# Input projections of a convolution and retention block as Strassen block products over both sequence halves

## The chip, the cores and the metric

The kernel runs on one core of one Trainium2 chip. The metric is the device time of one launch in microseconds (us), the median of three runs. The engines are named as in the profile: PE (TensorE), DVE (VectorE), ACT (ScalarE), POOL (GpSimd) and SP (the engine that issues most of the transfers).

## What is computed

The input x has 1024 tokens of 1024 channels, all in float32.

```
h = rmsnorm(x) * norm_gain
a_val, a_glu, a_gate, q, k, v, r_gate, g_a, g_b = split(h @ w_in)      # 1024 x 11264
u = causal_conv31(a_val * sigmoid(a_glu)) + bias                       # per channel
y_a = (silu(layernorm(u)) * silu(a_gate)) @ w_conv_proj
o = retention(rotary(q), rotary(k) / 16, v)        # 4 heads, dk 256, dv 512, chunks of 128
y_b = (normalised per head(o) * gain * silu(r_gate)) @ w_ret_proj
out = rmsnorm(x + (sigmoid(g_a) * y_a + sigmoid(g_b) * y_b) @ w_out) * final_gain
```

Retention goes chunk by chunk: a chunk's output is its own masked scores times v, plus q times a state of 256 x 512, and the chunk's k and v then go into the state.

## The kernel before

Every float32 operand of a large product is split into two float32r parts, high and low: ACT copies the value to float32r (high), DVE or POOL subtracts that from the value (low). `mm3` (L107) makes one block product from three matmuls: high by high, high by low, low by high. A matmul has 128 rows, 128 columns of weights and 512 moving columns.

The sequence is worked in two halves of 512 tokens, one after the other (`Half`, L186). A half first holds h, transposed, as eight tiles of 128 channels in two parts. Then it goes through its four heads (`head`, L365): four groups of products for q and k (24 matmuls each, `proj_c`, L263), rotary on DVE (L296 to L299) and POOL (L300, L301), groups of the gated convolution input, the output projection of the head before (`ret_proj`, L553), v (`proj_t`, L273), and four chunks. Between two chunks stand the 24 matmuls of the gate r for the next one (`rg_part`, L532). After the heads come the gates, the layer norm, `conv_proj` and `out_proj`.

A weight tile is 128 x 1024 values, loaded by SP (L145) and split by ACT and DVE (L161, L162); each tile of w_in is loaded and split once per half. Products read h from SBUF and leave their results there: of the results only the state of each head goes to memory, between the halves.

The 31 taps of the convolution are DVE instructions on 512 columns (L347), queued in `taps` and let out a few at a time after each group of products (`flush`, L738 to L741). The groups are emitted in the order of the list `groups`; within that, a scheduler at build time fixes each engine's order by its own estimate of what is ready, so that neighbouring instructions of one engine can change places. At run time every engine and every queue goes through its instructions in that order, and waits at the first one whose inputs or buffers are not ready.

## Time and profile before

| | |
|---|---|
| time, median of 3 runs | 1478.68 us (1478.56 to 1479.04) |
| span of the profiled execution | 1477.6 us |
| PE busy | 1452.9 us, 98% |
| DVE busy | 1082.1 us, 73% |
| ACT busy | 519.3 us, 35% |
| POOL busy | 229.1 us, 16% |
| moved by DMA | 150.79 MB, 102 GB/s |
| granted PE clock | 0.999 of full speed |

Busy time is an average over the whole span. A busy PE can still be waiting inside: matmuls are pipelined and their ends are modelled, so the number of matmuls in a stretch says more than the busy time. In a row of merged instructions (x3, x24) the time runs from the start of the first to the end of the last; the distance from one start to the next is what an instruction costs its engine, and it is shorter than the duration shown.

### The profile page before, as it was taken

Reading aid. Unit: us, or ns where it says so; the run is one execution under the profiler, and the core shown is the slowest. Engines: PE = TensorE matmul, PEld = TensorE weight load, DVE = VectorE, ACT = ScalarE, POOL = GpSimd, SP = SyncE. Lnnn points to the kernel's source line nnn. Section 1 sums busy time; section 2 is a strip of 40 time slices with the busy share of each in tenths; the row PEclk is TensorE's granted clock in tenths of the full one; section 3 lists DMA queues with packets and bytes.
Section 4 is the critical chain, followed back from the end, with each engine's and each line's share of the span. In section 5 each row is a group of like instructions: output and inputs, shape, how many; then the busy total and the mean of one; then the engine's idle time right before and its main releaser. Section 6 shows DMA issues by size and latency. Waiting matters only on the chain.

```text
span 1477.6 us, 16740 instructions
## 1 busy us (share of the span) xinstructions
PE 1452.9 (98%) x6564; PEld 1203.5 (81%) x6564; DVE 1082.1 (73%) x1422; ACT 519.3 (35%) x696; POOL 229.1 (16%) x167
## 2 busy tenths in 40 slices
PE   7999999999999999999999999999999999999998
PEld 5788888888888888888888888878878888888886
DVE  4848986998898896436579969978677759944443
ACT  5333243234233243533332432342341441345321
POOL 0303102112100032120220030120020000311100
PEclk9999999999999999999999999999999999999999
DMA  8214332232231243333552132132331322432331
GB/s 292 81 62 136 107 114 86 72 114 67 91 114 58 71 140 104 99 99 101 213 181 76 55 103 91 52 108 67 97 94 64 114 72 72 131 110 95 93 126 57
DMA packets 43135, 150.79 MB, mean 102 GB/s; under 512 B 4784, under 2 KB 5424, under 8 KB 43056
## 3 DMA queue, kind: packets, MB, share of 16 engines
q1 hardware_dynamic: 40752, 143.43, 30.2%
q10 hardware_dynamic: 2304, 6.29, 1.1%
q8 instruction: 51, 0.84, 0.2%
q14 instruction: 28, 0.23, 0.1%
HBM read 143.41 MB, written 6.29 MB: 101 GB/s over the span
## 4 chain that ended last, share of the span: by engine, by line
PE 84%; DVE 10%; DMA 3%; issue 1%; ACT 1%; POOL 0%; SPq 0%; DVEq 0%; POOLq 0%; ACTq 0%
PE ps L105 83%; DVE cv L347 4%; DVE w L162 2%; PE ps L524 1%; DMA raw<-w_glu 1%; DMA xn<-x 1%; ACT w L161 1%; DMA x<-xT 0%; DVE phl L495 0%; DVE x L251 0%; DVE o L516 0%; PE ps L448 0%; DVE v L471 0%; DVE p L490 0%; DMA raw<-w_rg 0%
## 5 line engine op out<-in xcount | busy, mean ns | idle before, releaser
L105 PE MATMUL ps<-h,w 128*128 128x512 f32 x2688 | 620.4, 392 | 11.0 <-ACT h L229 11.0
L105 PEld LDWEIGHTS ps<-h,w 128*128 128x128 f32 x2688 | 504.8, 188 | 116.9 <-ACT h L229 11.0
L347 DVE SCALAR_TENSOR_TENSOR cv<-u,small,cv 128x512 f32<-128x512 f32 x480 | 365.0, 786 | 5.7
L105 PE MATMUL ps<-w,h 128*128 128x512 f32 x1536 | 357.4, 391 | 0.0
L161 ACT CAST w<-raw 128x1024 fp32r<-128x1024 f32 (+1 forms) x207 | 213.4, 1041 | 350.6 <-PE ps L105 226.6
L105 PEld LDWEIGHTS ps<-w,h 128*128 128x128 f32 x1536 | 286.6, 188 | 58.7
L162 DVE TENSOR_TENSOR w<-raw,w 128x1024 fp32r<-128x1024 f32 (+1 forms) x210 | 272.0, 1306 | 66.2 <-ACT w L161 65.5
L105 PE MATMUL ps<-oT,w 128*128 128x512 f32 x768 | 175.4, 389 | 0.0
L105 PEld LDWEIGHTS ps<-oT,w 128*128 128x128 f32 x768 | 144.2, 188 | 29.9
L105 PE MATMUL ps<-w,m 128*128 128x512 f32 x384 | 87.7, 390 | 0.0
L105 PE MATMUL ps<-u,w 128*128 128x512 f32 x384 | 87.4, 389 | 0.0
L105 PEld LDWEIGHTS ps<-u,w 128*128 128x128 f32 x384 | 72.1, 188 | 15.0
L105 PEld LDWEIGHTS ps<-w,m 128*128 128x128 f32 x384 | 71.9, 188 | 14.8
L511 DVE BATCH_NORM_STATS2 bs<-ps 128x6 f32<-128x512 f32 x32 | 22.3, 696 | 74.0 <-PE ps L105 73.8
L164 ACT ACTIVATE w<-raw,small 128x1024 fp32r<-128x1024 f32 x32 | 36.9, 1152 | 99.2 <-PE ps L105 63.9
L127 POOL TENSOR_TENSOR rr<-rs,neg_half 128x1 f32<-128x1 f32 (+1 forms) x34 | 19.7, 578 | 325.6 <-DVE rs L124 325.6
L165 DVE SCALAR_TENSOR_TENSOR w<-raw,small,w 128x1024 fp32r<-128x1024 f32 x32 | 47.7, 1492 | 17.9 <-ACT w L164 17.9
L494 ACT CAST phl<-p 128x512 fp32r<-128x512 f32 x48 | 29.8, 621 | 71.4 <-DVE p L490 45.2
L439 POOL TENSOR_TENSOR shl<-s,shl 128x512 fp32r<-128x512 f32 x8 | 12.1, 1517 | 263.4 <-ACT shl L438 175.5
L584 POOL TENSOR_TENSOR yb<-yb,g 128x512 f32<-128x512 f32 x16 | 30.4, 1914 | 120.7 <-ACT g L582 120.6
L624 DVE TENSOR_TENSOR cv<-cv,w_ag 128x512 f32<-128x512 f32 x16 | 11.1, 693 | 49.5 <-ACT w_ag L592 49.5
L627 POOL TENSOR_TENSOR u<-cv,u 128x512 fp32r<-128x512 f32 x16 | 29.0, 1816 | 98.2 <-ACT u L626 74.2
(109 smaller groups left out, 1118.3 us busy)
## 6 DMA issues: line engine op xcount, KB each, us to landing
raw<-w_v SPq DMA_DIRECT2D x32, 512.0 KB, 3.5
raw<-w_rg SPq DMA_DIRECT2D x32, 512.0 KB, 4.0
raw<-w_ret SPq DMA_DIRECT2D x32, 512.0 KB, 3.6
raw<-w_k SPq DMA_DIRECT2D x16, 512.0 KB, 3.6
raw<-w_glu SPq DMA_DIRECT2D x16, 512.0 KB, 3.7
raw<-w_val SPq DMA_DIRECT2D x16, 512.0 KB, 4.3
raw<-w_gb SPq DMA_DIRECT2D x16, 512.0 KB, 3.5
raw<-w_ga SPq DMA_DIRECT2D x16, 512.0 KB, 3.5
```

Source lines behind the costliest of these rows:

```text
L105: nc.tensor.matmul(ps, lhsT=l, rhs=r, start=start, stop=stop)
L127: nc.gpsimd.tensor_tensor(r[:, :n], s[:, :n], neg_half[:, :n], ALU.pow)
L161: nc.scalar.copy(w[:, 0, sl], t[:, sl])
L162: nc.vector.tensor_tensor(w[:, 1, sl], t[:, sl], w[:, 0, sl].bitcast(F32), ALU.subtract)
L164: nc.scalar.activation(w[:, 0, :], t, AF.Copy, scale=gain)
L165: nc.vector.scalar_tensor_tensor(w[:, 1, :], t, gain, w[:, 0, :].bitcast(F32), ALU.mult, ALU.subtract)
L347: nc.vector.scalar_tensor_tensor(o, u[:, k:k + T], cw[:, cb, k:k + 1], o, ALU.mult, ALU.add)
L494: nc.scalar.copy(hi[:, d, :], st["p"][:, d, :])
L511: nc.vector.bn_stats(stats, ps)
L524: nc.tensor.transpose(ps[:, e * P:(e + 1) * P], o[:, e * P:(e + 1) * P], ident)
L584: nc.gpsimd.tensor_tensor(y, y, g, ALU.mult)
L627: nc.gpsimd.tensor_tensor(u[:, 1, :], d, u[:, 0, :].bitcast(F32), ALU.subtract)
```

## The change

The product h @ w_in is done in a first phase for all 1024 tokens. A pair of weight tiles (256 output columns, or 128 of glu with 128 of val) with the two halves of the tokens and the two halves of the 1024 input channels makes a 2 x 2 block product. The Winograd form of Strassen's rule computes it in seven products of 12 matmuls instead of eight. Its sums of weight blocks are made per pair on DVE, those of h once at the start. Partial sums are seeded in PSUM: a product adds onto what ACT or DVE, or an earlier product, left in the bank.

There are 44 pairs. Their results (q and k after rotary, v, the gates after their activation, the convolution after its taps) are stored to memory. The taps now work on 1024 columns, 1.2 of them per product. In the second phase each half loads what it needs from there; v and the gate r come with channels in the partitions, so v is transposed on PE. The retention keeps its chunks, but the decay is applied to the scores' mask, to k and to q instead of in the rotary tables. `ret_proj` of the head before, and `out_proj` of the first half, are spread between the items of a head as fillers. The rms sums of h are taken from the transposed x with one-column matmuls.

```
+N_U = 32
+N_V = 8
+W_HEAD = 4
+W_CLOSE = 6
+SPLIT_AHEAD = 4
+TAPS_PER_SLOT = 1.2
...
+        def load(self):
+            self.N = U("N")
+            nc.sync.dma_start(self.N, a[self.n1[0]][self.n1[1]])
+            self.X, self.Y = U("X"), U("Y")
+            w = a[self.n2[0]][self.n2[1]]
+            nc.sync.dma_start(self.X[:, T:], w[:, :T])
+            nc.sync.dma_start(self.Y[:, :T], w[:, T:])
...
+            def split(x, names):
+                n = len(names)
+                hi, lo = U("wh", F32R, (P, n, T)), U("wl", F32R, (P, n, T))
+                x = x.rearrange("p (n t) -> p n t", t=T)
+                nc.scalar.copy(hi, x)
+                nc.vector.tensor_tensor(lo, x, hi.bitcast(F32), ALU.subtract)
...
+            def s1():
+                nc.vector.tensor_tensor(X[:, :T], X[:, T:], Y[:, :T], ALU.add)
+                split(N, ["A11", "A12"])
+            def s1_split():
+                w = U("ws", F32R, (P, 2, T))
+                nc.scalar.copy(w[:, 0, :], X[:, :T])
+                nc.vector.tensor_tensor(w[:, 1, :], X[:, :T], w[:, 0, :].bitcast(F32), ALU.subtract)
...
+            def g2():
+                self.G = U("G")
+                nc.vector.tensor_tensor(self.G.rearrange("p (n t) -> p n t", t=T), X.rearrange("p (n t) -> p n t", t=T),
+                                        N[:, :T].unsqueeze(1).broadcast_to([P, 2, T]), ALU.subtract)
+            def g2_split():
+                split(self.G, ["S2", "S3"])
+            def s4():
+                nc.vector.tensor_tensor(Y[:, T:], N[:, T:], self.G[:, :T], ALU.subtract)
+            def y_split():
+                split(Y, ["A22", "S4"])
...
+        def run(self, slot):
+            pa, px = psum(), psum()
+            def product(ps, w, h, seeded):
+                wh, wl = self.op[w]
+                for k in range(4):
+                    sl = slice(k * P, (k + 1) * P)
+                    hh, hl = hop[h][k]
+                    mm3(ps, wh[:, sl], wl[:, sl], hh, hl, k == 0 and not seeded, k == 3, seeded)
+            o1, o2 = U("o1", F32, (P, 2, T)), U("o2", F32, (P, 2, T))
+            s5 = o2[:, 1, :]
+            product(pa, "A11", "B11", False)
+            pb = psum()
+            nc.scalar.copy(pb, pa)
+            slot()
+            product(px, "S1", "T1", False)
+            nc.scalar.copy(s5, px)
+            slot()
+            product(pa, "S2", "T2", True)
+            pd = psum()
+            nc.vector.tensor_tensor(pd, pa, s5, ALU.add)
+            slot()
+            product(pb, "A12", "B21", True)
+            self.use.c11(pb, o1, o2)
+            slot()
+            product(pa, "S3", "T3", True)
+            nc.scalar.copy(px, pa)
+            nc.vector.tensor_tensor(s5, pa, s5, ALU.add)
+            slot()
+            product(pd, "S4", "B22", True)
+            self.use.c12(pd, o1, o2)
+            slot()
+            product(px, "A22", "T4", True)
+            self.use.c2(px, o1, o2)
+            slot()
...
+    class Rope:
+        def first(self, ps, o1, i):
+            cos, sin = cs[i][:, 0, :], cs[i][:, 1, :]
+            nc.vector.tensor_tensor(o1[:, i, :], ps, cos, ALU.mult)
+            nc.vector.tensor_tensor(self.m[i][:, 0, :], ps, sin, ALU.mult)
+        def second(self, x, o1, o2, i):
+            cos, sin = cs[i][:, 0, :], cs[i][:, 1, :]
+            nc.vector.tensor_tensor(self.m[i][:, 1, :], x, sin, ALU.mult)
+            nc.vector.tensor_tensor(o2[:, i, :], x, cos, ALU.mult)
+            nc.gpsimd.tensor_tensor(o1[:, i, :], o1[:, i, :], self.m[i][:, 1, :], ALU.subtract)
+            nc.gpsimd.tensor_tensor(o2[:, i, :], o2[:, i, :], self.m[i][:, 0, :], ALU.add)
...
+    for j in (0, 1):
+        normed(0, j)
+    h_split("B11", b11, nc.gpsimd)
+    for p in prep[:2]:
+        p()
+    for j in (0, 1):
+        normed(1, j)
+    sums(b11, b12, b11, ALU.subtract)
+    h_split("T1", b11, nc.vector)
...
+    for i, p in enumerate(pairs):
+        if i + 2 < len(pairs):
+            pairs[i + 2].load()
+        steps = deque(pairs[i + 1].prep() if i + 1 < len(pairs) else [])
+        def slot():
+            if steps:
+                steps.popleft()()
+            carry[0] += TAPS_PER_SLOT
+            flush(int(carry[0]))
+            carry[0] -= int(carry[0])
+        p.run(slot)
+    flush(len(taps))
...
+            def values(c0):
+                def go(w):
+                    for c in range(c0, c0 + 2):
+                        ps = psum()
+                        for e in range(4):
+                            nc.tensor.transpose(ps[:, e * P:(e + 1) * P],
+                                                st["vT"][e // 2][:, e % 2, c * P:(c + 1) * P], ident)
...
+            items = [(keys, 1.5), (values(0), 1), (values(2), 1)] + [(chunk(c), 3.4) for c in range(NC)]
+            fillers = list(fillers)
+            share = len(fillers) / len(items)
+            done = 0
+            for i, (f, cost) in enumerate(items):
+                add(f, cost=cost, limit=W_HEAD)
+                while done < len(fillers) and done < round((i + 1) * share):
+                    fillers[done]()
+                    done += 1
```

In the order of the pairs, a convolution pair stands ahead of every fourth other pair, eight times; per head come the pairs of k, q, v, v, and the two of the gate r. The layer norm's four steps stand among the fillers of the last head of a half, and its application between the eight parts of that head's `ret_proj`.

## Rows read from the trace of the kernel before

**Rows 1.** The page: span, and busy time of PE.
```profile
span 1477.6 us, 16740 instructions
PE 1452.9 (98%) x6564; PEld 1203.5 (81%) x6564; DVE 1082.1 (73%) x1422; ACT 519.3 (35%) x696; POOL 229.1 (16%) x167
```

**Rows 2.** Groups by line and shape: the products of w_in; count, busy, mean ns.
```profile
L105 PE MATMUL ps<-h,w 128*128 128x512 f32 x2688 | 620.4, 392 | 11.0 <-ACT h L229 11.0
L105 PE MATMUL ps<-w,h 128*128 128x512 f32 x1536 | 357.4, 391 | 0.0
```

**Rows 3.** ACT in time, gates of half 0: start us, duration us, instruction.
```profile
621.34 0.60 ACT L592 ACTIVATE w_ag<-ps 128x512 f32<-128x512 f32 x1 [2.39 <-PE ps L105]
...
643.10 0.60 ACT L592 ACTIVATE w_ag<-ps 128x512 f32<-128x512 f32 x1 [3.39 <-PE ps L105]
```

**Rows 4.** PE in time, from the start to its steady run.
```profile
10.97 21.21 PE L105 MATMUL ps<-h,w 128*128 128x512 f32 x78 [10.97 <-ACT h L229]
...
32.83 26.10 PE L105 MATMUL ps<-h,w 128*128 128x512 f32 x114
58.77 5.60 PE L105 MATMUL ps<-w,h 128*128 128x512 f32 x24
...
68.70 1.63 PE L105 MATMUL ps<-w,h 128*128 128x512 f32 x6
```

**Rows 5.** The chain that ended last: its first pieces with x and the row factors.
```profile
3.54 7.36 DMA x<-xT
...
22.41 1.03 POOL r L127
```

**Rows 6.** DVE in time: instructions back to back, of 512 columns and of 1024.
```profile
441.61 0.69 DVE L471 TENSOR_TENSOR v<-ps,v 128x512 fp32r<-128x512 f32 x1
442.21 0.74 DVE L347 SCALAR_TENSOR_TENSOR cv<-u,small,cv 128x512 f32<-128x512 f32 x1
442.87 0.69 DVE L471 TENSOR_TENSOR v<-ps,v 128x512 fp32r<-128x512 f32 x1
...
747.06 2.35 DVE L162 TENSOR_TENSOR w<-raw,w 128x1024 fp32r<-128x1024 f32 x2
...
753.27 1.22 DVE L162 TENSOR_TENSOR w<-raw,w 128x1024 fp32r<-128x1024 f32 x1
```

**Rows 7.** Groups by line and shape: taps, and a DVE instruction of their kind on 1024 columns.
```profile
L347 DVE SCALAR_TENSOR_TENSOR cv<-u,small,cv 128x512 f32<-128x512 f32 x480 | 365.0, 786 | 5.7
...
L165 DVE SCALAR_TENSOR_TENSOR w<-raw,small,w 128x1024 fp32r<-128x1024 f32 x32 | 47.7, 1492 | 17.9 <-ACT w L164 17.9
```

**Rows 8.** DVE and POOL in time where both read SBUF, and the same DVE instruction alone.
```profile
735.59 3.54 DVE L679 SCALAR_TENSOR_TENSOR res<-res,rv,fg 128x512 f32<-128x512 f32 x2
...
735.51 2.40 POOL L284 TENSOR_TENSOR csd<-cs,decay 128x1024 f32<-128x1024 f32 x1
...
745.72 1.42 DVE L679 SCALAR_TENSOR_TENSOR res<-res,rv,fg 128x512 f32<-128x512 f32 x2 [0.72 <-POOL rv L675]
```

**Rows 9.** Groups by line and shape: the first POOL subtraction of rotary.
```profile
L300 POOL TENSOR_TENSOR qk<-rp 128x512 f32<-128x512 f32 x16 | 20.7, 1293 | 113.8 <-DVE rp L298 106.4 <-issue 7.4
```

**Rows 10.** Busy time by stretch: PE, PEld, DVE, ACT, POOL, then clock, DMA share, GB/s.
```profile
360.00:460.00 100.00, 99.93 (x459) 82.85 (x458) 91.08 (x122) 28.88 (x35) 12.39 (x11) 1.00 0.32 100
```

**Rows 11.** All engines in time around the end of a chunk (state update, transposes, gate).
```profile
227.10 0.60 PE L524 MATMUL ps<-ident,o 128*128 128x128 f32 x4
227.32 0.68 DVE L490 SCALAR_TENSOR_TENSOR p<-p,ps 128x512 f32<-128x512 f32 x1
227.46 5.71 PE L105 MATMUL ps<-w,h 128*128 128x512 f32 x24
...
228.34 0.62 ACT L494 CAST phl<-p 128x512 fp32r<-128x512 f32 x1
228.63 1.29 DVE L495 TENSOR_TENSOR phl<-p,phl 128x512 fp32r<-128x512 f32 x2
```

**Rows 12.** PE in time at the end of the span.
```profile
1459.75 10.81 PE L105 MATMUL ps<-w,m 128*128 128x512 f32 x47
```

More of the change, by code (lines that the diff above doesn't have):

```diff
@@ L128, in rsqrt, with flush @@
         return r
+    taps = deque()
+    def flush(n):
+        while taps and n > 0:
+            taps.popleft()()
+            n -= 1
+    nc.gpsimd.memset(ones, 1.0)
+    nc.gpsimd.memset(invd, 1.0 / D)
+    nc.gpsimd.memset(neg_half, -0.5)
+    zero = const("zero", [P, P], F32R)
+    nc.gpsimd.memset(zero.bitcast(F32), 0.0)
+    zrow = sb.tile([P, T], F32R, tag="t", bufs=N_T, name="zrow")
+    nc.gpsimd.memset(zrow.bitcast(F32), 0.0)
+    for _ in range(8):
+        mm(psum(), zero, zrow, True, True)
@@ new lines, in hybrid_block_kernel, with h_split @@
+    pairs = []
+    for i, p in enumerate(rest):
+        if i % 4 == 0 and i // 4 < NK:
+            cb = i // 4
+            pairs.append(Pair(("w_glu", cb), ("w_val", cb), Conv(cb)))
+        pairs.append(p)
+    hop = {}
+    v_left = [N_V]
+    def h_split(name, xs, eng):
+        ks = []
+        for x in xs:
+            if v_left[0] > 0:
+                v_left[0] -= 1
+                t = V("h", (P, 2, 2, T))
+                hi, lo = t[:, 0], t[:, 1]
+            else:
+                hi, lo = U("h", F32R, (P, 2, T)), U("h", F32R, (P, 2, T))
+            nc.scalar.copy(hi, x)
+            eng.tensor_tensor(lo, x, hi.bitcast(F32), ALU.subtract)
+            ks += [(hi[:, k, :], lo[:, k, :]) for k in range(2)]
+        hop[name] = ks
@@ new lines, in hybrid_block_kernel @@
+    for j in range(4):
+        load_x(0, j)
+    nc.sync.dma_start(small, a["small"])
+    nc.sync.dma_start(ident, a["ident"])
+    for j in range(4):
+        load_x(1, j)
+        if j == 1:
+            pairs[0].load()
+    cs = []
+    r_rows = []
+    for hf in range(2):
+        ps = psum()
+        for j in range(4):
+            q = U("sq", F32, (P, 2, T))
+            nc.scalar.activation(q, xt[hf][j], AF.Square, scale=D ** -0.5)
+            for k in range(2):
+                for c in range(NC):
+                    mm(ps[:, c:c + 1], q[:, k, c * P:(c + 1) * P], ones[:, 0:1],
+                       j == 0 and k == 0 and c == 0, j == 3 and k == 1, True)
+        r4 = rsqrt(ps[:, :NC], NORM_EPS, NC)
+        mm(ps, zero, zrow, True, True)
+        r_rows.append(bcast_rows(r4))
@@ new lines, in hybrid_block_kernel @@
+    sums(b21, b21, b11, ALU.subtract)
+    h_split("T4", b21, nc.vector)
+    for i in range(2):
+        t = U("cs", F32, (P, 2, T))
+        nc.sync.dma_start(t, a["cs"][i])
+        cs.append(t)
+    nc.sync.dma_start(dmask, a["dmask"])
+    nc.sync.dma_start(xi, a["xi"])
+    pairs[1].load()
+    carry = [0.0]
+    for i, p in enumerate(pairs):
[9 more added lines that the diff above has]
+        p.run(slot)
@@ L703, in finish @@
[L703 to L706 removed]
+            return lambda: add(go, [("w_out", 4 * eh + kp, None) for kp in range(4)] if c == 0 else [],
+                               4 if c == NC - 1 else 0)
     halves = [Half(0), Half(1)]
[L709 to L710 removed]
+    late = []
     for hv in halves:
+        hv.m, hv.res, hv.u2, hv.ss = [], [], [], []
@@ L719, in hybrid_block_kernel @@
+            hv.head(h, fill)
+        todo = list(range(NK))
+        for g in hv.ret_proj(H - 1):
+            if todo:
+                add(lambda w, hv=hv, cb=todo.pop(0): hv.ln_apply(cb), cost=0)
+            g()
+        for j in range(4):
+            hv.gate_b(j)
+        for db in range(NK):
+            hv.conv_proj(db)
+        late = [hv.out_proj(eh, c) for eh in range(2) for c in range(NC)]
+    for g in late:
+        g()
     for g in groups:
         ws.seq += g.weights
-    carry = 0.0
```

649 lines of the change are left out of this document (267 added, 382 removed).

## The prediction, made before the changed kernel was built or run

> **What bounds the kernel now.** I read the page first: PE is busy for 1452.9 of 1477.6 us [rows 1]. Busy time alone doesn't say that PE works at its pace, so the second view is the groups by line and shape, for the number of matmuls: the products of w_in are 2688 + 1536 = 4224 of 512 columns [rows 2], and the code makes 1968 others of that shape (768 in `ret_proj`, 384 each in `conv_proj` and `out_proj`, 432 in the chunks). The third is ACT in time where it does nothing but take results of `proj_c`: five gates start over 21.76 us, so 24 matmuls take 5.44 us and one takes 0.2267 us [rows 3]. Then 6192 matmuls are 1403.7 us of the 1477.6. PE's matmul count is the bound. The remaining 73.9 us hold the start, the small products and transposes, the waits between and the tail. At the start the 216 matmuls issued before 68.70 us would take 49.0; with some 4 us of small products PE has lost about 16 us by then [rows 4]. After its last matmul at 1470.56 the span lasts 7 us more [rows 12]. The rest of the span has little idle time; even in a stretch of 100 us in which DVE is busy for 91.1, PE goes on at its pace, with 459 records in 99.9 us [rows 10].
>
> So a cut in matmuls comes off the end, as long as nothing else takes its place. The change cuts matmuls and gives DVE, the next engine, a larger and a tighter part.
>
> **Products removed.** 44 pairs by 7 by 12 are 3696 matmuls in place of 4224: 528 fewer, 528 x 0.2267 = -119.7 us. A product of 12 takes 2.72 us, a pair 19.04, the phase 838.
>
> **Transposes of v.** 32 chunks each gain four of 128 columns. Four of the same kind delay the next product from 227.10 to 227.46, 0.36 us [rows 11]: 32 x 0.36 = +11.5 us.
>
> **Start.** Before, PE begins at 10.97 with h not yet normed [rows 4]. Now the seven sums of h must be made first, and pair 0 can't end before the last of them (T4). x is there from 10.9 us, and the row factors were known at 23.4 before [rows 5]; with sums of squares by one-column matmuls I take 20 for the first half. From there DVE has 16 normings of 512 columns at 0.66, 8 sums and 8 low parts of 1024 at 1.13, and the seven preparations of pair 0, 6.3 us (below): 35 us. The prices are the distances between starts: 0.60 for 512 columns, 0.66 with a scalar from a tile, 2.35 - 1.22 = 1.13 for 1024 [rows 6]. Three of the seven operands have their low parts on POOL, six of 2.40 us [rows 8]. While POOL reads SBUF, DVE's instructions with two SBUF inputs stretch: a couple takes 3.54 us instead of 1.42 beside a POOL instruction of 2.40 [rows 8]. I put 10 of these 14.4 us on DVE's path, since the normings take one input from PSUM. T4 is then ready at about 65 and pair 0 ends at 66, where 19 were its due: 47 lost instead of 16, +31 us. The ends: without collisions and with a first product overlapping, 37 lost (+21); with factors at 23.4 and every collision paid, 56 (+40).
>
> **DVE in the first phase.** A pair costs DVE four instructions of 1024 (low part of N, the sum G, its low part, low part of Y) and three of 512 (two sums, low part of S1), 4 x 1.13 + 3 x 0.60 = 6.32, plus two additions on partial sums, 1.20: 7.52 us. Taps come at 1.2 x 7 = 8.4 a pair while there are any, 31 last 3.7 pairs out of five. A tap of 1024 columns isn't in the trace. From below it is 0.66 + 0.53 = 1.19; 0.76 busy per tap now (365.0/480) gives 1.29; the like instruction on 1024 has a mean of 1.49 [rows 7]. I take 1.25: 10.5 us a pair. A plain pair with taps is 18.0 us of DVE against 19.04 of PE. It fits, and what hides it is that six of the seven products leave time between the sums that PE waits for. PE's tight point is `pd`: product five may not write the bank until DVE has added `s5`, so a DVE behind by more than 2.72 - 0.60 = 2.1 us stops PE.
>
> The eight rotary pairs don't fit: 8 x 0.60 = 4.8 more on DVE, and four POOL instructions of 1.29 [rows 9], 5.2 us in which DVE's two-input work may stand. k and q come one after the other and meet taps in all four heads. At the full price a pair is 7.52 + 10.5 + 4.8 + 5.2 = 28.0, 9 too many; two in a row less the slack of 2.1 are 15.9, and 12.6 for the two heads where the taps run out in q: 57 us in all. With half of POOL's time it is 36; the other end is 0, if the order of the queues lets PE take products of the next pair. I take +23: the stretch of rows 10, where a DVE at 91% held nothing up, is nearer than the full price, though its load is an average and this comes in lumps.
>
> The Trainium skill (SBUF — State Buffer, "SBUF: two separate sides") says that the port pair DVE and GpSimd share is an exclusive lock for a whole instruction, so that the loser blocks. Rows 8 bear that out: 2.12 of 2.40 us came on DVE. By that rule alone the rotary pairs would cost 57 us instead of 23; it is the sharper part of the second rival.
>
> **Transfers.** Each pair loads 1 MB and stores 1 MB (convolution pairs half), 88 MB or so in 850 us, no more per us than now (102 GB/s). Loads are issued two pairs ahead, some 19 us, so I cost them at nothing. On SP's queue they stand behind stores that wait for a pair's last results, at most one pair; the cover goes if buffers run short. By my count the 32 U buffers are just full at a pair's start (h 12, cos and sin 2, two pairs of loads 6, operands 7, results 4, convolution 1), so the next operands wait for the stores before, some 6 us, and still have 10 to spare.
>
> **Second phase.** PE has about 505 us of work. Four things take the place of the products that hid the rest. (a) Between kv and the next chunk's product with the state PE had 24 matmuls. The state takes from the kv's end to 228.63 + 1.29 = 229.92, 2.8 us after PE went on at 227.10 [rows 11], 3.2 with the two halves in one instruction. Fillers are 2.72 each, but none stands between chunks 0 and 1: 2.5 us x 6 heads, and 3 gaps in the first head of all, which has no fillers: 22. (b) That head also waits for its first loads, 5. (c) At six head changes four w_ret tiles are split at once, when the last filler has let go of them; 2 each, 12. (d) The layer norm stands beside a head's full DVE load: its 15 subtractions and sums are 9 us of DVE, seven sums on POOL another 9, chained; 8 a half, 16. Together 55; the build-time order can move ready products forward, as it does now, which I credit with 10, and the waits that were in the middle before go, about 10. Net +35, with ends of +5 (all gaps filled) and +70 (nothing filled, the layer norm at twice that).
>
> **Sum**, on the profiled execution: 1477.6 - 119.7 + 11.5 + 31 + 23 + 35 = 1458.4. The median of the runs is 1.1 us above the span: 1459.5, so 1460 us. With every term at its better end it is 1396, at its worse end 1537.
>
> **Rivals.**
> (1) The gaps close: the build-time order pulls ready products into every wait. For it: the 99.9 us in rows 10. Against: the start can't be filled. Start +25, rotary 0, second phase +12: 1407 us. Chance 0.22.
> (2) DVE becomes the bound of the first phase, and the change is slower. Place: the pairs with taps. It decides from a tap of (19.04 - 7.52)/8.4 = 1.37 us on. At 1.49 [rows 7] a plain pair is 20.0, 1 us over for some 26 pairs, 26; with rotary at its full 57 the phase loses 83 instead of 23: 1520 us, or 1500 with a tap at the edge. For it: rows 8, and DVE's largest share yet. Against: taps are cheaper than 1.37 wherever they are alone. Chance 0.20.
> (3) The second phase opens up: the state's chain, the weights and the layer norm at +75 instead of +35: 1500 us. For it: no long run of independent products is left in a head. Against: fillers, and a whole `out_proj` in the second half's first head. Chance 0.13.
> That the products aren't saved is no rival: the count is in the code.
>
> **Chances.** My forecast's case, 1435 to 1485, has 0.45. A difference of 0.2% (3 us) is about what can be told from none. Of the forecast's case 0.39 is faster by more than that, 0.05 the same, the rest slower; with rival 1, faster 0.61, with a little of 2 and 3 the same 0.06, slower 0.33. The range is 1405 to 1515: it leaves out the better end of rival 1 and the worse of 2.
>
> **What would show it.** Right: 3696 matmuls of the pairs at 0.227 us between results; pair 0 ending near 66 us; PE idle mostly in the first 66 us, in the eight rotary pairs, and at heads' chunk 0 and layer norm. DVE near 95% in pairs with taps, behind 80% after the last tap. Wrong: PE below 90% across plain pairs (rival 2); results of a pair more than 19.1 us apart without DVE busy, which would mean buffers or loads; idle PE above 70 us in the second phase (rival 3), or below 20 (rival 1).

## The result, and the profile after

The changed kernel takes 1574.52 us (median of four runs, 1573.98 to 1577.29) where the kernel before takes 1478.62: 1.0653 times as long, 95% interval 1.0638 to 1.0668. It is slower by 96 us; 1460 with a range of 1405 to 1515 was forecast. The profiled execution, the slowest of the four, has a span of 1575.5 us, 117 more than the 1458.4 of the sum.

The page of the changed kernel: span, busy time by engine, and three of its groups (busy us, mean ns, idle time before and its releaser).

```profile
span 1575.5 us, 16585 instructions
PE 1451.7 (92%) x6278; PEld 1168.9 (74%) x6278; DVE 1184.5 (75%) x1378; ACT 545.8 (35%) x761; POOL 215.6 (14%) x153
...
L108 PE MATMUL ps<-h,wh 128*128 128x512 f32 x2112 | 669.2, 398 | 31.1 <-DVE ps L234 13.4
...
L108 PE MATMUL ps<-h,wl 128*128 128x512 f32 x1056 | 418.7, 396 | 2.6 <-DVE wl L183 2.6
L333 DVE SCALAR_TENSOR_TENSOR cv<-u,small,cv 128x1024 f32<-128x1024 f32 x240 | 313.0, 1304 | 3.3
```

Against [rows 1], PE's busy time is the same with fewer matmuls, and its share fell from 98% to 92%. The products are there as counted: 2112 + 1056, and 528 more with S1, are the 3696 of the sum [rows 2]. A tap lasts 1.304 us in the mean, below the 1.37 from which rival 2 decides; DVE's share is 75% over the span and 89% in the stretch with the first taps and rotary pairs (100 to 200 below), so no long stretch has it as its bound. So the time went to three other places, which the stretches show (columns as in [rows 10]):

```profile
0.00:100.00 100.00, 70.02 (x233) 56.10 (x234) 58.23 (x62) 34.92 (x37) 25.52 (x19) 0.81 0.29 102
100.00:200.00 100.00, 92.73 (x391) 74.06 (x390) 89.08 (x90) 29.56 (x41) 16.33 (x9) 0.97 0.26 90
...
700.00:900.00 200.00, 200.00 (x869) 162.81 (x868) 158.27 (x159) 75.96 (x111) 0.00 (x0) 1.00 0.30 106
...
953.00:1576.00 623.00, 544.17 (x2444) 435.06 (x2442) 438.44 (x612) 213.20 (x301) 128.00 (x96) 0.94 0.42 142
```

**The start.** PE in time (start, duration, instruction, idle time before):

```profile
5.58 13.81 PE L108 MATMUL ps<-ones,sq 128*128 128x1 f32 x64
...
23.66 13.65 PE L108 MATMUL ps<-ones,sq 128*128 128x1 f32 x64
...
43.83 2.04 PE L108 MATMUL ps<-dg,ones 128*128 128x512 f32 x2 [5.48 <-DVE dg L119]
...
73.79 0.79 PE L108 MATMUL ps<-h,wh 128*128 128x512 f32 x1 [6.84 <-POOL h L374]
...
82.58 0.79 PE L108 MATMUL ps<-h,wh 128*128 128x512 f32 x1 [3.73 <-ACT wh L182]
87.88 1.22 PE L108 MATMUL ps<-h,wh 128*128 128x512 f32 x2 [4.50 <-DVE ps L234]
```

The one-column matmuls (the first two rows) of the two halves run one after the other, so the second half's row factors reach PE at 43.83; after that PE stands for the low parts on POOL (6.84), for a weight tile's high part on ACT (3.73) and for the first partial sum (L234, 4.50). The first product of pair 1 ends at 101.46, so pair 0 ends at about 98.7 and not at 66: some 80 us are lost where 47 were forecast. About 3 of them belong to this execution: in five of the variants below whose start is the same (x_align, x_fill, x_rope, x_noln, x_notap) that product ends at 98.6 to 99.0. What DVE and POOL do at that time, one fence for each engine:

```profile
57.99 2.36 DVE L408 TENSOR_TENSOR x<-x,x 128x1024 f32<-128x1024 f32 x2
...
65.77 2.36 DVE L408 TENSOR_TENSOR x<-x,x 128x1024 f32<-128x1024 f32 x2
...
73.77 6.68 DVE L408 TENSOR_TENSOR x<-x,x 128x1024 f32<-128x1024 f32 x2 [2.23 <-POOL h L374]
80.37 4.50 DVE L374 TENSOR_TENSOR h<-x,h 128x1024 fp32r<-128x1024 f32 x2
...
87.14 0.69 DVE L234 TENSOR_TENSOR ps<-ps,o 128x512 f32<-128x512 f32 x1
```

```profile
65.10 17.56 POOL L374 TENSOR_TENSOR h<-x,h 128x1024 fp32r<-128x1024 f32 x4 [21.89 <-ACT h L373]
```

The first and the last of these four on POOL by themselves:

```profile
65.10 8.63 POOL L374 TENSOR_TENSOR h<-x,h 128x1024 fp32r<-128x1024 f32 x1 [21.89 <-ACT h L373]
...
79.33 3.33 POOL L374 TENSOR_TENSOR h<-x,h 128x1024 fp32r<-128x1024 f32 x1
```

Two sums of 1024 columns on DVE take 2.36 us with POOL idle (57.99). The four low parts on POOL take 17.56 us together, 4.39 each in the mean and not the 2.40 of [rows 8], and it isn't always DVE that pays. POOL's first one lasts 8.63 us: while it is open, DVE goes through sums and low parts at their usual price (65.77) and pauses at 71.5, and PE waits for what POOL makes there. From 73.77 on DVE pays: its next two sums, for which PE is waiting too, take 6.68.

**The pace.** ACT in time, the copies that follow product one of three plain pairs:

```profile
782.29 0.57 ACT L227 COPY ps<-ps 128x512 f32<-128x512 f32 x1 [2.19 <-PE ps L108]
785.15 0.59 ACT L230 COPY o<-ps 128x512 f32<-128x512 f32 x1 [2.29 <-PE ps L108]
...
801.66 0.57 ACT L227 COPY ps<-ps 128x512 f32<-128x512 f32 x1 [4.91 <-PE ps L108]
...
821.03 0.57 ACT L227 COPY ps<-ps 128x512 f32<-128x512 f32 x1 [2.19 <-PE ps L108]
```

A pair takes 19.37 us, with PE busy all the time at full clock (the stretch from 700 to 900), and not 19.04. Products one to four take about 2.80 us each, five to seven 2.72.

**The second phase.** It begins at 953.60 and lasts 621.9 us. What PE waited for in it (us in total, times, longest us):

```profile
PE ps L640 <- DVE o L633: 17.1, 12, 4.3
PE ps L108 <- POOL acc L709: 15.6, 2, 9.1
PE ps L108 <- DVE oT L648: 9.9, 5, 3.6
PE ps L108 <- ACT v L584: 9.5, 1, 9.5
PE ps L108 <- DVE dg L119: 8.5, 2, 4.2
```

None of these waits is longer than 9.5 us, and no engine is full: DVE is busy for 438 of 623 us, PE for 544. The waits name short chains (a chunk's normed output o, the layer norm's sum and row factors, the values of v in the first head) and each stands where PE has nothing else next in its queue.

### The profile page after: what moved, and what is told of

Its sections match the earlier page's. It is cut to its first block, busy times and chain, and to the rows that moved or that the text cites. A ratio compares the mean times of both kernels' runs of the same rounds, so it can differ in the third digit from the quotient of the medians.

```text
span 1575.5 us, 16585 instructions
## 1 busy us (share of the span) xinstructions
PE 1451.7 (92%) x6278; PEld 1168.9 (74%) x6278; DVE 1184.5 (75%) x1378; ACT 545.8 (35%) x761; POOL 215.6 (14%) x153
## 4 chain that ended last, share of the span: by engine, by line
PE 48%; DVE 7%; issue 3%; POOL 3%; DMA 1%; ACT 1%; SPq 0%; POOLq 0%; DVEq 0%; ACTq 0%
PE ps L108 47%; DVE w L485 1%; POOL acc L709 1%; DVE o L633 1%; POOL rr L129 1%; PE ps L640 1%; DVE p L603 1%; DVE bs L628 1%; DVE acc L723 1%; DVE phl L612 1%; PE ps L581 0%; DMA raw<-w_ret 0%; POOL q L566 0%; DVE oT L648 0%; DMA gb<-gb_d 0%
## 5 line engine op out<-in xcount | busy, mean ns | idle before, releaser
L108 PE MATMUL ps<-h,wh 128*128 128x512 f32 x2112 | 669.2, 398 | 31.1 <-DVE ps L234 13.4
L108 PEld LDWEIGHTS ps<-h,wh 128*128 128x128 f32 x2112 | 401.4, 191 | 130.2 <-DVE ps L234 16.8
L108 PE MATMUL ps<-h,wl 128*128 128x512 f32 x1056 | 418.7, 396 | 2.6 <-DVE wl L183 2.6
L333 DVE SCALAR_TENSOR_TENSOR cv<-u,small,cv 128x1024 f32<-128x1024 f32 x240 | 313.0, 1304 | 3.3
L108 PEld LDWEIGHTS ps<-h,wl 128*128 128x128 f32 x1056 | 200.9, 190 | 48.5 <-DVE wl L183 3.1
L108 PEld LDWEIGHTS ps<-oT,w 128*128 128x128 f32 x768 | 148.0, 196 | 53.6 <-DVE oT L648 11.3
L108 PE MATMUL ps<-h,ws 128*128 128x512 f32 x528 | 133.0, 400 | 2.6 <-ACT h L373 1.6
L108 PEld LDWEIGHTS ps<-h,ws 128*128 128x128 f32 x528 | 100.5, 191 | 27.8 <-ACT h L373 2.1
L183 DVE TENSOR_TENSOR wl<-G,wh 128x1024 fp32r<-128x1024 f32 x44 | 53.8, 1223 | 48.1 <-ACT wh L182 48.1
L183 DVE TENSOR_TENSOR wl<-N,wh 128x1024 fp32r<-128x1024 f32 x44 | 55.9, 1270 | 30.6 <-ACT wh L182 19.2
L182 ACT CAST wh<-N 128x1024 fp32r<-128x1024 f32 x44 | 46.2, 1049 | 55.6 <-POOL o L291 48.7
```

Source lines behind the costliest of these rows:

```text
L108: nc.tensor.matmul(ps, lhsT=l, rhs=r, start=start, stop=stop, skip_group_check=onto)
L182: nc.scalar.copy(hi, x)
L183: nc.vector.tensor_tensor(lo, x, hi.bitcast(F32), ALU.subtract)
L333: nc.vector.scalar_tensor_tensor(o, u[:, k:k + S], cw[:, cb, k:k + 1], o, ALU.mult, ALU.add)
```

## The experiments

The times are medians; ratios are to the kernel before, which ran beside them (1477.7 to 1478.8 us). Edits are to the changed kernel unless it is said otherwise.

**x_eight: the products alone.** A pair by the eight plain products, in the same two phases.
```diff
-            product(pa, "A11", "B11", False)   # seven products, sums between
+            product(px, "A21", "B12", True)    # eight products, no sums
+            product(px, "A22", "B22", False)
...
```


> The changed kernel with the pairs' seven products replaced by the plain eight (no sums of blocks of h or of the weights, everything else as in the changed kernel, taps at 1.05 a product so that a pair gets as many). Theory 'the products are saved, the phases cost': each pair is one product longer, 44 x 2.77 = 122 us, less some 20 us of the start without sums and some 20 of the rotary pairs, which DVE then has time for: 1640 to 1665 us. Rival 'the sums eat the saving': the seven-product form with its sums takes about as long as eight plain products; then 1560 to 1600 us.

1656.02 us, 1.1195 [1.1174, 1.1215]: 81.5 us more than with seven. Its plain pairs take 22.40 us, eight times 2.80, against 19.37. 44 times 3.03 is 133 us of products saved; some 50 of them go back where the eight products lose less: 28 in the start (pair 0 ends at 73.7 with one product more) and 22 in the rotary pairs, which all take 22.40. With as many products as the kernel before it is 178 us slower than that: this is what the two phases cost with nothing saved.

**x_align and x_phase: the pace.** x_align makes the tiles behind the small parameters begin at multiples of 128 bytes; x_phase places two small groups of tiles ahead of U.
```diff
-    small = const("small", [P, N_SMALL])
+    small = const("small", [P, N_SMALL + 8])       # x_align
+    for tag in ("rs", "rr"):                       # x_phase, ahead of U's first tile
+        pre = sb.tile([P, NC], F32, tag=tag, bufs=6, name=f"{tag}_pre")
```


> The changed kernel with 32 more bytes per partition in the table of small parameters, so that the tiles behind it start at multiples of 128 bytes, as they did before the change. In the changed kernel the four products of a pair that take h from the V tiles last 2.80 us and the three that take it from U tiles 2.73. Theory 'address': these tiles' start address slows the matmuls; then all seven take 2.72, which is 44 x 4 x 0.07 = 12 us, and some 6 more in conv_proj and out_proj: 1555 to 1560 us. Rival 'place or traffic': what slows them is where V lies or what goes on beside it; then nothing moves, 1573 to 1577 us.

1575.82 us, 1.0656 [1.064, 1.0672], pairs still 19.37 us: alignment was not it.

> Two small groups of tiles (384 bytes in all) are placed ahead of the U tiles instead of between the U and the V tiles, so that the distance from U to V in SBUF becomes 131,072 bytes, a multiple of 4096, as it was in the kernel before (126,976). Nothing else changes. Theory A (products are slower, 2.80 us per 12, because the low bits of the addresses of the two operands differ): products one to four of a pair fall from 2.80 to 2.72 us, conv_proj and out_proj from 44.95 to 43.6 us per 192; a plain pair 19.37 to 19.1; 12 us less in the first phase, 5 in the second: 1555 to 1560 us. Rival (the pace has another cause, such as the number of stores and loads beside it): 1573 to 1577 us, 2.80 as before.

1562.96 us, 1.0566 [1.0541, 1.0591]. ACT in time in x_phase, at the copies after product one (L230 here):

```profile
775.15 0.57 ACT L230 COPY ps<-ps 128x512 f32<-128x512 f32 x1 [2.12 <-PE ps L108]
...
794.19 0.57 ACT L230 COPY ps<-ps 128x512 f32<-128x512 f32 x1 [4.84 <-PE ps L108]
...
813.23 0.57 ACT L230 COPY ps<-ps 128x512 f32<-128x512 f32 x1 [2.12 <-PE ps L108]
```

19.04 us to the hundredth, in the plain pairs away from rotary. The last pair's first product ends 9.8 us earlier (927.47 for 937.23), the span is 12.8 shorter: the distance of the two groups of tiles sets the pace, as theory A has it, and the median came 3 us above its range. Which low bits of the addresses count isn't shown.

**x_start and x_start2: the start.**
```diff
-                    mm(ps[:, c:c + 1], q[:, k, c * P:(c + 1) * P], ones[:, 0:1], ...)  # 64 a half
+                nc.vector.tensor_tensor(qs, qs, q, ALU.add)                           # then 4 a half
-    h_split("B11", b11, nc.gpsimd)        # B21 and B22 too
+    h_split("B11", b11, nc.vector)
+            if i == 0 and first_steps:    # x_start2: one sum of h after each product
+                first_steps.popleft()()
```


> The changed kernel with the squares of a half summed on DVE before the one-column matmuls (4 products of them in place of 32 a half), and with the low parts of B11, B21 and B22 on DVE instead of POOL. Theory 'late row factors': the start is long because PE takes 14 us for the squares of each half one after the other, so that the second half's factors come at 44 us, and because POOL and DVE then block each other; pair 1's first product would end near 72 us in place of 101.5, and the kernel takes 1543 to 1550 us. Rival 'DVE's own chain of sums': DVE's work for the seven operands binds, and taking POOL's 14 us on adds what the factors save; then 1565 to 1575 us.

1563.24 us, 1.0573 [1.0556, 1.0591]. Pair 1's first product ends at 87.78. DVE in time in x_start, its last pieces before product five may go on:

```profile
68.03 1.21 DVE L411 TENSOR_TENSOR x<-x,x 128x1024 f32<-128x1024 f32 x1
69.16 2.47 DVE L374 TENSOR_TENSOR h<-x,h 128x1024 fp32r<-128x1024 f32 x2
71.55 0.68 DVE L188 TENSOR_TENSOR X<-X,Y 128x512 f32<-128x512 f32 x1
72.15 1.22 DVE L183 TENSOR_TENSOR wl<-N,wh 128x1024 fp32r<-128x1024 f32 x1
73.28 0.68 DVE L194 TENSOR_TENSOR ws<-X,ws 128x512 fp32r<-128x512 f32 x1
73.89 0.69 DVE L234 TENSOR_TENSOR ps<-ps,o 128x512 f32<-128x512 f32 x1
```

Without POOL a low part takes 1.2 us, but DVE is one solid chain, and the partial sum (L234) stands behind all of it: products five to seven come after the whole preparation.

> x_start (squares summed on DVE ahead of one matmul per column block, low parts of B11, B21 and B22 on DVE) with one more edit: the sums of h and their low parts are issued one after each product of pair 0, and pair 1's preparation after pair 0's last product, so that the addition on the first partial sum (pd), for which product five waits, stands in DVE's queue in its turn and not behind the whole chain. Theory: in x_start PE stood idle from 54 to 74 us for that order alone; pair 1's first product ends 8 to 12 us earlier than in x_start (87.78), at 76 to 80, and the time is 1551 to 1556 us. Rival: DVE's work of the start is one solid chain whatever its order, pair 1's first product ends at 86 to 89 and the time is 1562 to 1565.

1561.6 us, 1.0564 [1.0549, 1.058]. Pair 1's first product ended at 79.85, as the theory had it, and pair 43's at 922.11 against 923.31 in x_start. 7.9 us were gained and 6.5 of them had gone back by pair 4, most likely because the work put off was still DVE's.

**x_rope, x_notap and x_slack: taps and rotary.**
```diff
-            carry[0] += TAPS_PER_SLOT
+            carry[0] += 0.3 if isinstance(p.use, Rope) else 1.15                  # x_rope
-            taps.extend(tap(k) for k in range(1, TAPS))                           # x_notap
-            pd = psum()
+            pe, pd = psum(), psum()                                               # x_slack
+            nc.scalar.copy(pe, pa)
             nc.vector.tensor_tensor(pd, pa, s5, ALU.add)
-            product(pa, "S3", "T3", True)
+            product(pe, "S3", "T3", True)
```


> First phase only: 0.3 taps per product in the eight rotary pairs and 1.15 in the others, instead of 1.2 in all until they run out; the number of taps is the same. Theory (22 us of the first phase are lost where rotary and taps come together on DVE): the first phase ends 12 to 20 us earlier than 953.6 and the time is 1555 to 1563 us. Rival (the eight rotary pairs lose time to their own chain, POOL and partial sums, and not to taps): the first phase ends within 4 us of 953.6, 1571 to 1577 us.

1578.32 us, 1.0684 [1.0666, 1.0702]: no gain. The build-time order put more of the taps in threes on DVE (3.9 us in a piece, 29 such groups for 21); the losses moved to other pairs and kept their sum, 836.3 us from pair 1 to pair 43 for 835.8. So this run doesn't settle the theory.

> 30 of the 31 taps of the convolution are left out (its first multiplication and the stores stay), so DVE has 240 instructions of 1.30 us less in the first phase. In the changed kernel the 42 pairs after the second lose 22 us, all within three pairs of a rotary one. x_rope spread the taps otherwise, but at build time they were grouped in threes, so it settled nothing. Theory (the 22 us come where taps and rotary meet on DVE): 5 us or less are left of the 22, and the time is 1552 to 1560 us. Rival (the rotary pairs' own chain, with POOL and the partial sums, costs them with no taps at all): 15 us or more are left, 1567 to 1576 us.

1551.64 us, 1.0503 [1.0485, 1.052]. From pair 1 to pair 43 every pair takes 19.36 to 19.38 us, the rotary ones too; the stretch from 100 to 200 us, which had 391 matmuls, in x_notap:

```profile
100.00:200.00 100.00, 100.00 (x435) 81.35 (x435) 55.28 (x66) 32.93 (x47) 14.33 (x9) 1.00 0.31 105
```

With POOL's rotary work still there and no taps, nothing is lost: all of the 22 us came from rotary and taps together.

> One edit to the changed kernel: ACT copies the bank of product three to another bank, product five goes on there, and DVE's addition of the first partial sum (pd) reads the old bank. Product five then waits for ACT and no longer for DVE; pd is first needed by product six, one product (2.7 us) later. Theory (the 22 us of the rotary pairs are lost at pd, for which product five waits): 10 to 18 us less, 1557 to 1565 us. Rival (DVE has more work than fits beside the rotary pairs, and PE waits for it at the next place): under 5 us less, 1570 to 1577 us.

1560.52 us, 1.0559 [1.0543, 1.0575]: 14 us less, inside the theory's range, but the trace gives the theory less than half of the 22. What PE waited for from pair 1 to pair 43, first the changed kernel, then x_slack:

```profile
PE ps L108 <- DVE ps L234: 8.9, 6, 3.1
...
PE ps L108 <- ACT ps L227: 5.8, 5, 1.7
PE ps L108 <- ACT ps L234: 4.1, 2, 2.1
```

The wait for the partial sum is gone, and so are 8.9 us between the two pairs (826.9 for 835.8). The other 13.4 stay, and PE now waits for ACT's copies between banks. The rest of the 14 lies in the start, where pair 1's first product ends at 98.17, close to the other variants, and in the second phase.

**x_ln, x_fill and x_noln: the second phase.** x_ln moves the layer norm's steps to the second to last heads, x_fill the products that fill a head, x_noln leaves the statistics out.
```diff
-                more = [hv.ln_load, hv.ln_stats, hv.ln_var, hv.ln_rows]     # in the last head
+            extra = {1: {0: hv.ln_load}, 2: {0: hv.ln_stats, 4: hv.ln_var}, 3: {5: hv.ln_rows}}.get(h, {})  # x_ln
-                while done < len(fillers) and done < round((i + 1) * share):
+                for _ in range([0, 0, 2, 2, 1, 1, 2][i]):                   # x_fill
```


> The changed kernel with the layer norm's steps moved ahead: loads and sums beside the second head, squares and variance beside the third, its rows late beside the fourth, instead of all beside the fourth. Theory 'chained layer norm': of some 60 us that PE loses around the fourth head of the two halves most are the chain POOL sums, mean, squares, variance, rows, on which PE's queue waits; then 1530 to 1545 us. Rival 'DVE's load': the fourth head and the application are held by DVE's amount of work, and moving it fills other heads up: 1565 to 1575 us.

1564.17 us, 1.0572 [1.0555, 1.0589]. The 15.6 us of waits on POOL's sum are gone, but the waits for o, oT and v stay: between the two.

> Second phase only: the output products that fill a head are put behind the items of the head where the gaps are (two behind the third and the fourth item, one behind the fifth and sixth, two behind the last) instead of evenly, and w_ret isn't split during the first four items of the first head, where ACT stood behind it. No work is changed. Theory (the second phase loses to short chains that lack independent products at the right place): the first head's wait for v on ACT (9.5 us) goes and the heads' gaps shrink, 18 to 28 us less: 1547 to 1557 us. Rival (the losses belong to chains that no order of these products covers): only the wait on v goes, 1565 to 1572 us. Third possibility: the even spread was the better one, over 1576 us.

1559.95 us, 1.0557 [1.0541, 1.0573]: 14.6 us less, between the two and nearer to the theory. The wait for v fell from 9.5 us to 2.5, while that on POOL's sum for the layer norm grew from 15.6 to 32.4.

> The statistics of the convolution's layer norm are left out in both halves (seven sums on POOL, eight subtractions, squares and seven sums on DVE, the row factors); its loads, the multiplication (by a constant tile instead of the row factors), gates and the projections stay. In the second phase of the changed kernel the last head with its ret_proj and conv_proj took 138.6 and 138.9 us in the two halves, for 108.1 and 109.5 of PE work at its pace. Theory A (term d, the layer norm, is the one that was mis-sized: its chains on POOL and DVE cost most of these 60 us): 35 to 50 us less, 1525 to 1540 us. Rival (the last head loses the time to its own chunk chain, with too few products beside it): 8 to 20 us less, 1555 to 1567 us.

1544.49 us, 1.0439 [1.0415, 1.0463]: 30 us less. It is twice the 16 of my term, and half of the 60 that the last heads lose. PE's largest waits in what is left of the phase are for o, oT and v (22.9, 12.3 and 10.5 us), the heads' own chains; how the other half divides among them no run shows.

**x_all, x_spread: the gains together.** x_all has x_start2, x_phase, x_fill and the moved layer norm. x_spread adds two edits:
```diff
-        todo = list(pending) if g.cost else []
+            while pending and pending[0][0] >= 2:       # o's transposes two groups later
+                todo.append(pending.pop(0)[1])
-                at(2, hv.ln_stats)
+                    at(i + 1, lambda w, hv=hv, i=i: hv.ln_step(i))   # one block per item
```


> The edits that helped, together: squares summed on DVE, low parts of h on DVE and in turn with pair 0's products (x_start2), the two small groups of tiles ahead of U (x_phase), the fillers of the heads in other places (x_fill), and the layer norm's steps spread over the heads before (load in the second, statistics in the third, rows in the last). Theory (three separate losses: start, pace, second phase): the gains add up, 13 + 12 + 14 + about 10, to 1520 to 1532 us, still slower than before. Rival (they cover one another): 1538 to 1550 us.

1523.85 us, 1.031 [1.0295, 1.0325]: the gains add up. What PE waited for in its second phase, first line:

```profile
PE ps L663 <- DVE o L656: 35.2, 13, 10.1
```

The layer norm's block of 15 DVE instructions is now issued amid the chunks of the third head, ahead of their normed output.

> x_all (1523.85 us) with two edits in the second phase: the transposes of a chunk's output are issued two groups after the chunk instead of one, and the subtractions and squares of the layer norm are issued one block per item of the third and fourth head instead of all at once. Theory (what is left there is the order of short chains): the 35 us that PE waits for o fall below 12, 1500 to 1510 us. Rival (DVE is too full in these heads whatever the order): 1517 to 1526 us.

1496.24 us, 1.0122 [1.0107, 1.0137]: 27.6 us less for an order (the two edits weren't tried apart). The same line, and the whole second phase of x_spread:

```profile
PE ps L663 <- DVE o L656: 7.4, 6, 1.9
```

```profile
926.00:1497.00 571.00, 524.46 (x2444) 428.74 (x2442) 435.21 (x612) 211.51 (x303) 133.72 (x96) 0.97 0.46 155
```

With the same 2444 matmuls as in the changed kernel's row from 953 to 1576, the phase is 52 us shorter: 32 of them idle time of PE (78.8 to 46.5), 20 in its busy time, which are pace (x_phase) and clock (0.94 to 0.97).

**x_mix, x_best: two pairs by plain products.** Pairs 0 and 1 by eight products, the sums of h beside pair 1; x_mix has x_start2 and x_phase, x_best all edits.
```diff
+    plan = [[lambda: h_b("B21", b21, 0, (2, 3)), ...],
+            [lambda: h_t("T1", b11, b12, b11), lambda: h_t("T2", b11, b22, b11), ...]]
```


> x_start2 and x_phase together, and pairs 0 and 1 by the eight plain products, which need only the four blocks of h; the four sums of h are made beside pair 1. Two products more (5.4 us of PE). x_start2 and x_phase together would give some 1549 us. Theory (the start is long because pair 0 can't end before all seven operands of h are made): pair 2 ends its first product 15 to 25 us earlier than with these two, 1525 to 1536 us. Rival (DVE's norming chain alone sets the start): 1545 us or more.

1572.27 us, 1.0628 [1.0607, 1.0648]: the time says the rival, the place the theory. Pair 2's first product ends at 76.74, 23.6 us ahead of x_start2, and then most pairs of the first half take 20 to 21 us and some 23 to 28, with 22.9 us of waits for low parts (wl) and 13.8 for partial sums on DVE, whose taps begin two pairs later.

> All of it: x_spread with the plain products of x_mix in pairs 0 and 1 and the extra bank of x_slack. Theory (start, rotary pairs and second phase are separate losses): 1523.85 less 20, 12 and 18, 1468 to 1485 us, about the kernel before. Rival (what is taken from one place comes back at the next): 1495 to 1515 us.

1481.87 us, 1.003 [1.002, 1.0039], within the theory's range. With x_slack's bank the plain pairs are back at 19.04 us and the start's gain is kept.

**x_order, x_order2, x_order3: the pairs' order**, on x_best: v, k, v, q in each head; the same with fewer taps beside rotary; v, rg, k, v, rg, q.
```diff
-        rest.append((EightPair if h == 0 else Pair)(("w_k", 2 * h), ("w_k", 2 * h + 1), Rope(k_d[h])))
-        rest.append(Pair(("w_q", 2 * h), ("w_q", 2 * h + 1), Rope(q_d[h])))
-        for i in range(2):
+        for i, (n, d) in enumerate((("w_k", k_d), ("w_q", q_d))):
...
+            rest.append(Pair((n, 2 * h), (n, 2 * h + 1), Rope(d[h])))
-            carry[0] += TAPS_PER_SLOT
+            carry[0] += 0.7 if isinstance(p.use, Rope) else 1.0     # x_order2
```


> x_best (1481.87 us) with the pairs in another order: of each head a v pair, the k pair, the other v pair, the q pair, instead of k, q, v, v; pair 1 is then a v pair by plain products. Theory (two rotary pairs in a row are a lump of DVE work that pairs with slack would take up): 10 to 20 us less, 1462 to 1472 us, faster than the kernel before (1478). Rival (with 1.2 taps per product a plain pair has no slack to take it up): 0 to 6 us less, 1476 to 1482 us.

1476.59 us, 0.9983 [0.9974, 0.9992]: 5 us less than x_best and level with the kernel before; a sixth of a per cent is inside the 0.2% that I count as no difference.

> x_order with 0.7 taps per product in rotary pairs and 1.0 in the others. Theory (both are needed): another 5 to 12 us less than x_order, 1455 to 1468 us. Rival (the order alone does it, or the build-time order groups the taps again, as in x_rope): within 4 us of x_order.

1488.29 us, 1.0059 [1.0046, 1.0072]: worse than x_order by 12. PE waits for the partial sum 20.0 us in the first phase, for 7.9 in x_order; that the taps taken from the rotary pairs stand in lumps elsewhere, as in x_rope, is likely but not shown. x_order came out as its rival had it, and x_order2 as neither.

> x_order (1476.59 us) with the pairs of each head as v, rg, k, v, rg, q: two plain pairs between rotary ones, and a plain pair 2 beside the last sums of h. Theory (what is left in the first phase are lumps of DVE work): 6 to 14 us less, 1462 to 1471 us. Rival (the sums of h hold up pair 2 whatever it is, and the later single losses come where a convolution's taps begin): within 4 us of x_order.

1481.18 us, 1.0016 [1.0004, 1.0029]: no better than x_order, and 4.6 us above it just outside the rival's range. The losses moved to other pairs (26.57 us from pair 4 to 5, 24 to 25 at single ones later) and kept their sum: 816.9 us from pair 2 to pair 43, for 816.4.

## Why the prediction was wrong

The first phase was to end at 66 + 43 x 19.04 + 23 = 908 us; it ended at 953.6, 46 late. The second was to take the other 551 of the 1458.4; it took 622, 71 more. Together these are the 117 us. Two steps of the prediction failed, the start and the second phase, and a third term was a little off.

**Products removed: right in number, a little off in price.** The count stands. The 0.2267 us of [rows 3] is TensorE's pace for operands placed as they were before; in the new layout four products of seven ran at 0.2333. 0.33 us a pair is 14 us in the first phase. x_phase gave 9.8 back there, as its rotary pairs lose 4 more, and 12.8 in all. I had named a pair above 19.1 us without DVE busy as a sign of buffers or loads: it was neither.

**Start: the first step that failed, +64 in place of +31.** Two parts of it were wrong. I took 20 us for the row factors of the first half, which held, and nothing for the second's, whose 64 one-column matmuls queue behind the first's (5.58 to 37.3 us in all); DVE finished the last operand at 84.87 and not at 65. And I let pair 0 end one us after that, though the partial sum that product five needs stood behind all of it in DVE's order, so that three products came after it; the first of them took 5.3 us (87.88 to 93.16), at a granted clock of 0.50, the level of 1.2 GHz. The 10 us of collisions with POOL were about right: DVE's last sums and low parts were stretched by 6.5 us (6.68 for 2.36, 4.50 for 2.36), and it stood 2.2 for POOL. x_start, which takes away the late factors and POOL's part at once, gave back 13.7 us by pair 1's first product (11.3 in the median). In x_best, whose first two pairs need only the four blocks of h, pair 2's first product ends at 76.84; in the changed kernel it was 123.39 (101.46 + 21.93). Half of that came with the plain pairs (23.6, x_mix against x_start2): what cost most was to need all seven operands for the first pair.

**Rotary: the size came out, in part by luck.** 22 us were lost from pair 1 to pair 43 (835.8 less 42 x 19.37) for my 23, in the rotary pairs and just behind them, and x_notap shows that rotary and taps together make them. But 23 was picked between 0 and 57, and two prices were off. A tap costs DVE 1.20 us from start to start, not 1.25. And POOL's pieces make DVE's instructions beside them about 12 us longer than usual in all eight rotary pairs, 1.6 a pair and not 5.2 (five taps last 2.31 to 2.38 us where most last 1.28), while POOL's own 32 pieces take 62 us where 1.29 each would be 41. With the measured prices the prediction's sum at the full price gives about 25, my estimate. The tight point, `pd`, was the place of 8.9 of the 22 (x_slack). The Trainium skill (SBUF — State Buffer, "SBUF: two separate sides") says that the pair of ports shared by DVE and GpSimd is an exclusive lock, held for a whole instruction by whichever starts first. The trace agrees that one of them stands while the other works (8.63 us on POOL for 2.40, then 6.68 on DVE for 2.36); the 57 us took DVE to be the loser each time, and here POOL, which had the time, lost more. DVE in time in the second rotary pair of the changed kernel, a tap while POOL is idle and one beside POOL:

```profile
131.09 1.27 DVE L333 SCALAR_TENSOR_TENSOR cv<-u,small,cv 128x1024 f32<-128x1024 f32 x1
132.29 1.21 DVE L199 TENSOR_TENSOR G<-X,N 128x1024 f32<-128x1024 f32 x1
...
147.51 2.37 DVE L333 SCALAR_TENSOR_TENSOR cv<-u,small,cv 128x1024 f32<-128x1024 f32 x1
149.81 1.77 DVE L188 TENSOR_TENSOR X<-X,Y 128x512 f32<-128x512 f32 x1
```

**Second phase: the second step that failed, and the largest: +35 became about +100,** after the 3 us of pace that x_phase took from it. The layer norm was sized at 16 and cost 30 (x_noln). The state's chain, the first loads and the weights at the heads' changes, terms a to c, failed by a common assumption, as I read the waits; no run took them apart: I priced each gap as one wait less one filler of 2.72 us, and credited the build-time order with 10 us. But a queue runs in order: a filler helps only where it stands next on PE, and what PE waits for only comes if nothing long stands ahead of it on DVE. x_fill (15), x_ln (10) and x_spread (28) removed no work and gave back some 50 us; in x_spread, at x_phase's pace, the phase takes 570 us, for the 551 of the sum. So most of the 71 us is order, and +35 was some 20 too small even in the best order found. Nor had the sum a term for the clock: PE is busy for 544 us of the phase, 39 more than the 505 of work counted, and part of these is the lower clock after its waits (0.94 granted in the mean, 0.999 in the kernel before).

**The rivals.** Rival 3 named the phase, and its sign came (78.8 us of idle PE, over the 70); it was too small (+75). Rival 2 got the sign by a wrong mechanism: plain pairs did not lose to DVE. Rival 1's gaps did not close by themselves; its credit for a build-time order that pulls products into waits came from a kernel in which, as I see it, most of the 6192 matmuls were there to be pulled in at all times.

**What stays open.** x_order is level with the kernel before although 504 matmuls (114 us at 0.2267) are gone. By its trace the start still loses 31 us (pair 2's first product ends at 76.79, for 46.2 us of products), 36 are lost among the pairs (816.4 us from pair 2 to pair 43, for 41 x 19.04), where PE waits for partial sums, low parts and copies, and PE is idle for 46 us of the second phase. Whether heads among the pairs, as before, would close these was not tried.

## What to carry to other kernels

When a bound engine's work is cut and the rest is moved to a phase of its own, price the new phase by the order of each queue: for every short chain, what stands next on the bound engine while it runs, and what stands ahead of it on the engine that makes it. Fillers spread evenly are worth less than the same ones placed behind the chains; here that order was some 50 us. At a start, price the last operand that the first results need, with all that stands ahead of it in its engine's queue, and let a cheap plain form run until the operands of the clever one are made.

## What the runs showed of the hardware that was not expected

- A matmul of 512 columns took 0.2333 us or 0.2267 with the same shapes, at full clock and with PE never idle, by where its two operands lay: with 131,456 bytes between the two groups of tiles a product took 2.80 us, with 131,072 2.72. 384 bytes of small tiles moved gave every plain pair 0.33 us.
- Behind a wait of 6.4 us PE ran at the lower clock for a while, and so the wait cost more than its length. PE in time in the changed kernel, around the layer norm's sum in the last head, and the granted clock of two stretches of it (the figure behind POOL's):

```profile
1103.42 2.08 PE L108 MATMUL ps<-acc,invd 128*128 128x512 f32 x2 [6.44 <-POOL acc L709]
1104.51 4.53 PE L108 MATMUL ps<-oT,w 128*128 128x512 f32 x12
...
1110.93 2.88 PE L108 MATMUL ps<-oT,w 128*128 128x512 f32 x12
```

```profile
1103.50:1108.80 5.30, 5.30 (x14) 3.57 (x15) 3.27 (x6) 2.43 (x4) 0.00 (x0) 0.67 0.01 3
1108.90:1113.80 4.90, 4.90 (x22) 3.74 (x20) 4.90 (x9) 2.53 (x4) 0.00 (x0) 1.00 0.29 92
```

  The twelve matmuls behind the wait took 4.5 us where the next twelve of the same kind took 2.9, at full clock (1.00, 2.4 GHz); at a granted clock of 0.67 in the mean the first twelve ran mostly at 1.2 GHz.
- When DVE and POOL both worked on SBUF tiles without a pause, either could be the one that stood. A POOL subtraction of 1024 columns lasted 8.63 us instead of 2.40 while DVE ran at its usual pace, and the next sums on DVE 3.34 us each instead of 1.18.
